# Scores of three attention units moved between the input products, and later row sums in a trunk kernel

## The chip, the cores and the metric

The kernel runs on one core of a Trainium2 chip. The metric is the device time of one execution in microseconds (us). The engines are named as in the profile: PE (TensorE), DVE (VectorE), ACT (ScalarE), POOL (GpSimd) and SP (SyncE, which here only issues transfers). Each works through its own queue in order; semaphores tie the queues together.

## The reference

Two layers of a trunk over 256 latent tokens x and 256 context tokens, width 1024. Each layer is a half-step SwiGLU, a token mixer and a second half-step SwiGLU; each sub-layer norms its input, shifts and scales it by values of a conditioning vector, norms its output and gates it.

```python
def _token_mixer(h, hc, ...):
    q, k, v, u, gb, gc, z = jnp.split(h @ w_in, SPLITS, axis=-1)
    ...                                              # kc, vc, uc: of the context tokens
    attn = _window_attention(q, k, v, kc, vc, sink)  # 8 heads, 2 of k and v, window 128, plus context
    ssm, ssm_c = _s5_mixer(u, uc, ...)               # diagonal scan, both directions, then a gated unit
    conv = gb * _short_conv(gc * z, conv_w)          # three taps
    y = jnp.concatenate([attn, ssm, conv], axis=-1) @ w_out
    if not ctx_out:                                  # the last layer
        return y, None
    ...                                              # the same for the context tokens
x = x + _gated_post(y, norm_post[l, 1], m[:, 5])
x = x + MACARON * _ffn_sublayer(x, m, 2, *f1)
```

All data and weights are float32.

## The kernel before

Values lie with the channels on partitions and the 512 tokens along the free axis: first the context (0 to 255), then x. Of each channel block there are 128 rows. A float32 product is made of three products in a reduced float32: each factor is split into a high part (`xh`, `wh`, a rounding copy on ACT) and a low part (`xl`, `wl`, a subtraction on DVE, or on POOL for the weights of w_out), and PE adds high by high, low by high and high by low (helper at L157, `mm3`). Weights come by transfers on SP into a ring of four buffers `wr` (`RAW`), and their two parts go into rings of six (`WB`). SP issues in order, so a transfer that waits for a free buffer holds all behind it.

The order of PE's instructions is the order of the program (a manual schedule for PE alone); on the other engines the framework's scheduler sets it. In the mixers the program's order is a table, `PROG`, of one string for each layer; the mixer function reads it step by step and calls a function for each. The letters are:

- `t10`, `t8`, `t9`, `t12`, `t11`, `t13`: half a product with w_in (for two blocks of output channels); each name stands twice, once for each half. ACT copies the result out (`wi`, L1247); t12 and t9, t11 and t13 give the convolution its parts (POOL L1275, L1277, L1283 and DVE L1279, L1281; result `cv`, then split).
- `u`, `U`: regroup the scan's input. `s0`, `s1`: the states of the scan's two halves (PE `pe` L1055, ACT copies `tx` L1059, POOL L1072 and L1084, DVE L1074 to L1091). `o0`, `o1`: read out the states (PE `py` L1110, with weights in buffers of the ring `wr`). `b0`, `b1`: back to channels, with a gelu. `g`: the gated unit of the scan (`pglu` L1147, weight `wglu` loaded by SP).
- `q`, `k`: split q or k in high and low part. `v`: transposes of v.
- `Sn`, `Tn`, `Vn`: attention of unit n. In the first mixer there are twelve units, three for each of four pairs of heads: two blocks of 128 x tokens and one for the context tokens (n = 2, 5, 8, 11). `S` is scores (PE L1170), the row maximum (`mx`, DVE L1181), its negative times the scale (`nm`), exponentials with sums (ACT L1194), the sink (`es`, ACT L1196), sums and reciprocal (DVE L1198, L1200) and the division (`P`, ACT L1202). `T` is the transposes of P (PE `pt` L1212) and two copies out of PSUM, the first on ACT, the second on DVE (`PT`, L1217 and L1215). `V` is the product with v (PE `O` L1228) and the split of its result.
- `wd`, `Wd`: load and split block d of w_out (the split on POOL). `edks`: the part of output block d from input block k, in token span s (context or x); the sum goes to PSUM `po`. `yd`: copy out and square. `x0`, `x1`: begin a norm and the residual. `z`: go one step further in the first span's chain (first a sum over the residual's squares by PE, `ss` L344, then its row factor `rb` L337 and the norm for the next SwiGLU).
- `r` (second mixer): one step of the row-wise part, among them transposes of x (`pxr` L439).

At the end of the first mixer the last two `z` are the sum over the squares of the residual x (`xacc` on DVE, `xsq` on ACT) and the row factor with the next SwiGLU's input. In the mixers P and most other values take a slot of a common pool of 39 (`SLOTS`).

Of the kernel before, what the change touches and what calls it, by code (L numbers as in the profile page):

```python
# [45 lines left out]
QSPLIT = (True, False)  # L46

PROG = (
# [13 lines left out]
)  # L62
QP = ()
LPF = 4
TORD = (ENG.Activation, ENG.DVE)
# [13 lines left out]
class Trunk:  # L79
# [1075 lines left out]
            cat[6 + half] = ch, cl  # L1155


    def attn_s(self, l, i, q, k, qt):
        nc = self.nc
        S = [self.ps("S") for _ in range(2)]  # L1160
        for part in ((qt,) if qt is not None else (0, 1)):
            for ab in range(2):
                pr = slice(64 * ab, 64 * ab + 64)
                if qt is not None:
                    o, qo = S[ab], CTX + qt * 128
                else:
                    o, qo = S[ab][:, part * 256:part * 256 + 256], part * 128
                xy = ((0, 0), (1, 0), (0, 1)) if len(q) > 1 else ((0, 0),)
                for n, (x, y) in enumerate(xy):
                    nc.tensor.matmul(o, q[x][pr, qo:qo + 128], k[y][pr, :o.shape[1]], start=n == 0,  # L1170
                                     stop=qt is None and n == len(xy) - 1, skip_group_check=True, tile_position=(64 * ab, 0))
        if qt is not None:
            c = 384 if qt == 0 else 256
            for ab in range(2):
                nc.tensor.matmul(S[ab][:, c:c + 128], self.identb, self.trib[:, qt], start=False, stop=True,
                                 skip_group_check=True)
        n = 1 if qt is not None else 2
        w = 512 // n
        mx = self.tiny("mx", 4)
        for ab in range(2):  # L1180
            nc.vector.tensor_reduce(mx[:, n * ab:n * ab + n], S[ab].rearrange("p (n k) -> p n k", n=n), axis=AX.X,  # L1181
                                    op=OP.max)

        sink = self.misc[:, l, 4 * i:4 * i + 2 * n] if n == 2 else self.misc[:, l, 4 * i:4 + 4 * i:2]
        cols = [slice(j, j + 1) for j in range(2 * n)]
        nm, es, sm = (self.tiny(t, 4) for t in ("nm", "es", "sm"))
        for c in cols:
            nc.vector.tensor_scalar(nm[:, c], mx[:, c], -SCALE, sink[:, c], op0=OP.mult, op1=OP.min)
        for c in cols:
            nc.vector.tensor_scalar(es[:, c], nm[:, c], sink[:, c], None, op0=OP.subtract)  # L1190
        Pm = [self.slot("P") for _ in range(2)]
        part = lambda j: Pm[j // n][:, j % n * w:j % n * w + w]
        for j in range(2 * n):
            nc.scalar.activation(part(j), S[j // n][:, j % n * w:j % n * w + w], AF.Exp, bias=nm[:, j:j + 1],  # L1194
                                 scale=SCALE, accum_out=sm[:, j:j + 1])
        nc.scalar.activation(es[:, :2 * n], es[:, :2 * n], AF.Exp)  # L1196
        for c in cols:
            nc.vector.tensor_scalar(sm[:, c], sm[:, c], es[:, c], None, op0=OP.add)  # L1198
        rd = self.tiny("rd", 4)[:, :2 * n]
        nc.vector.reciprocal(rd, sm[:, :2 * n])  # L1200
        for j in range(2 * n):
            nc.scalar.activation(part(j), part(j), AF.Copy, scale=rd[:, j:j + 1])  # L1202
        return Pm
# [33 lines left out]
    def mixer(self, l, H, pend, newH):  # L1237
        nc, a = self.nc, self.a
        last = l == NL - 1
        both = self.spans  # L1240
        lo = CTX if last else 0
        ev, cat = {}, {}
# [54 lines left out]
        u = [ev[0], ev[1]]  # L1297
        U, ut, vt = [], [], self.slot("vt")

        def vtok():  # L1300
            pv = self.pm("pvt")
            for tt in range(4):
                nc.tensor.transpose(pv[:, tt * 128:(tt + 1) * 128], ev[3][:, tt * 128:(tt + 1) * 128], self.ident)
            nc.scalar.activation(vt, pv, AF.Copy)
# [35 lines left out]
        qs, ks = {}, []  # L1340

        def qsplit(i):
            qs[i] = self.split(ev[4 + i], lo, T, pool=i in QP)

        def ksplit():
            ks.extend(self.split(ev[2], 0, T))

        wr, yr, us, q = {}, {}, [], []
# [25 lines left out]
        P, PT = {}, {}  # L1374

        def attn_s(n):
            i, qt = units[n]
            if not QSPLIT[last]:
                qs[i] = ev[4 + i],
            P[n] = self.attn_s(l, i, qs[i], ks if QSPLIT[last] else (ev[2],), qt)  # L1380

        def early_out(n):
            if last:
# [9 lines left out]
            v=lambda n: vtok(), k=lambda n: ksplit(), q=qsplit,  # L1393
            s=lambda n: S.append(self.ssm_states(l, n, U)), o=lambda n: yt.append(self.ssm_out(l, n, U, S[n], lo)),
            b=lambda n: G.append(self.ssm_back(yt[n], lo)), w=weight, r=lambda n: next(rows, None),
            g=lambda n: self.ssm_glu(l, G, cat, lo), e=early_out, x=tail if last else bound, S=attn_s,
            y=lambda n: oevac(n // 10, n % 10), z=lambda n: self.advance(out[0][1]), W=weight,
            T=lambda n: PT.update({n: self.attn_t(P.pop(n), units[n][1])}),
# [244 lines left out]
```

## Time and profile before

| | us |
|---|---|
| median of 3 runs | 1796.78 |
| lowest and highest run | 1795.67, 1804.11 |
| the profiled execution, its own time | 1789.94 |
| its span, first to last instruction | 1788.1 |

| engine | busy us | share of the span |
|---|---|---|
| PE | 1696.9 | 95% |
| DVE | 1111.6 | 62% |
| ACT | 687.6 | 38% |
| POOL | 728.3 | 41% |

The mean granted clock of PE is 0.982 of full speed (2.4 GHz). The share of busy time is a mean over all stages. The first mixer begins at 482.3 us of the span and ends at about 657.5, the second begins at about 1466; in between lie products of the SwiGLUs.

In a timeline a line has the start in us, the time in us, the engine, the line of the kernel, the operation, what it writes and reads, how many instructions are taken together, and in brackets how long the engine stood idle before it and what released it. A busy PE at half its clock counts as busy, so the granted clock stands in a view by stretch.

### The profile page before, as it was taken

The page shows a single profiled execution, that of the slowest core. Times are in us where ns is not written, and L with a number is a line of the kernel's source. Part 1 is how long each engine was busy: PE and PEld are TensorE (multiplying, and loading weights), DVE is VectorE, ACT ScalarE, POOL GpSimd, SP SyncE. Part 2 cuts the span into 40 slices and gives each one's busy share as a digit, 9 for nine tenths or more (in the row PEclk, how much of TensorE's full clock was granted, in tenths as well). Part 3 has the DMA queues.
Part 4 walks back from the last instruction along what each step waited for, and adds up shares of the span by engine and source line. Part 5 has one row for each costly group of instructions (what it writes and reads, how often), then busy time and mean ns, then how long its engine had stood idle before and what let it go on. Part 6 is the DMA issues. An engine that isn't in the chain of part 4 may idle for free.

```text
span 1788.1 us, 28686 instructions
## 1 busy us (share of the span) xinstructions
PE 1696.9 (95%) x11040; PEld 1449.6 (81%) x11040; DVE 1111.6 (62%) x2222; ACT 687.6 (38%) x1225; POOL 728.3 (41%) x651
## 2 busy tenths in 40 slices
PE   7999999999987989999999999999999989899998
PEld 5787777898975889787888989888888978579997
DVE  5798886827486466777774276765456476753223
ACT  4332322325337644323222244322222444655443
POOL 3100898955453143553438353000000563446552
PEclk9999999999998999999999999999999999999999
DMA  8676656644144032756664332646466443445662
GB/s 287 217 228 197 211 169 194 219 131 130 37 148 148 25 95 62 218 169 206 180 199 141 109 119 83 224 139 202 130 198 226 125 140 115 147 157 187 198 189 94
DMA packets 101688, 285.92 MB, mean 160 GB/s; under 512 B 19904, under 2 KB 27152, under 8 KB 101552
## 3 DMA queue, kind: packets, MB, share of 16 engines
q1 hardware_dynamic: 98960, 276.57, 49.1%
q0 software_dynamic: 2304, 7.46, 1.1%
q8 instruction: 86, 1.41, 0.3%
q14 instruction: 50, 0.41, 0.1%
q10 hardware_dynamic: 288, 0.07, 0.0%
HBM read 270.45 MB, written 15.70 MB: 160 GB/s over the span
## 4 chain that ended last, share of the span: by engine, by line
PE 79%; DVE 9%; issue 4%; DMA 4%; ACT 3%; POOL 1%; SPq 0%; DVEq 0%; ACTq 0%; POOLq 0%
PE pgu L157 39%; PE pd L157 18%; PE sk L157 8%; PE yr L497 4%; PE po L157 3%; DVE junk L252 2%; DVE wl L135 1%; DMA wr<-in_w_ada_dram 1%; PE pw L157 1%; PE ss L344 1%; DVE tn L370 1%; ACT wh L132 1%; POOL wl L135 1%; PE O L1228 1%; ACT hh L372 1%
## 5 line engine op out<-in xcount | busy, mean ns | idle before, releaser
L135 POOL TENSOR_TENSOR wl<-wr,wh 128x1024 fp32r<-128x1024 f32 (+1 forms) x140 | 327.8, 2359 | 674.9 <-ACT wh L132 324.6
L132 ACT ACTIVATE wh<-wr 128x1024 fp32r<-128x1024 f32 (+2 forms) x350 | 342.3, 983 | 594.5 <-PE pgu L157 166.4
L157 PE MATMUL pgu<-hh,wh 128*128 128x512 f32 (+1 forms) x1296 | 468.2, 361 | 0.0
L157 PE MATMUL pgu<-hl,wh 128*128 128x512 f32 (+1 forms) x1296 | 464.3, 358 | 0.0
L157 PE MATMUL pgu<-hh,wl 128*128 128x512 f32 (+1 forms) x1296 | 464.0, 358 | 0.0
L252 DVE SCALAR_TENSOR_TENSOR junk<-wr,sb 128x1024 bf16<-128x1024 f32 x224 | 314.4, 1404 | 161.3 <-DMA wr<-in_w_ada_dram 159.2
L135 DVE TENSOR_TENSOR wl<-wr,wh 128x1024 fp32r<-128x1024 f32 (+1 forms) x210 | 250.4, 1194 | 57.8 <-ACT wh L132 56.4
L157 PEld LDWEIGHTS pgu<-hh,wh 128*128 128x128 f32 x1296 | 244.3, 188 | 41.8 <-issue 1.7
L157 PEld LDWEIGHTS pgu<-hl,wh 128*128 128x128 f32 x1296 | 244.5, 189 | 40.4 <-issue 0.5
L157 PEld LDWEIGHTS pgu<-hh,wl 128*128 128x128 f32 x1296 | 244.2, 188 | 40.3
L157 PE MATMUL pd<-xh,wh 128*128 128x512 f32 (+1 forms) x696 | 241.8, 347 | 4.3 <-ACT xh L628 4.3
L157 PE MATMUL pd<-xl,wh 128*128 128x512 f32 (+1 forms) x696 | 237.4, 341 | 1.4 <-DVE xl L629 1.4
L157 PE MATMUL pd<-xh,wl 128*128 128x512 f32 (+1 forms) x696 | 237.2, 341 | 0.0
L157 PEld LDWEIGHTS pd<-xh,wh 128*128 128x128 f32 x696 | 131.6, 189 | 22.2 <-ACT xh L628 5.3
L157 PEld LDWEIGHTS pd<-xl,wh 128*128 128x128 f32 x696 | 132.0, 190 | 19.3 <-DVE xl L629 2.5
L157 PEld LDWEIGHTS pd<-xh,wl 128*128 128x128 f32 x696 | 131.6, 189 | 16.5
L157 PE MATMUL sk<-hl,wh 128*128 128x256 f32 x480 | 136.5, 284 | 6.8 <-DVE hl L375 6.8
L157 PE MATMUL sk<-hh,wh 128*128 128x256 f32 x480 | 137.5, 286 | 4.5 <-ACT hh L372 4.5
L157 PE MATMUL sk<-hh,wl 128*128 128x256 f32 x480 | 135.6, 283 | 0.0
L628 ACT ACTIVATE xh<-pgu 128x512 fp32r<-128x512 f32 (+1 forms) x61 | 35.1, 575 | 180.4 <-DVE pgu L627 180.3
L157 PEld LDWEIGHTS sk<-hl,wh 128*128 128x128 f32 x480 | 92.7, 193 | 8.4 <-DVE hl L375 8.3
L157 PEld LDWEIGHTS sk<-hh,wh 128*128 128x128 f32 x480 | 92.2, 192 | 6.2 <-ACT hh L372 6.1
(384 smaller groups left out, 2472.7 us busy)
## 6 DMA issues: line engine op xcount, KB each, us to landing
wr<-in_wgu_dram SPq DMA_DIRECT2D x170, 512.0 KB, 4.2
wr<-in_w_ada_dram SPq DMA_DIRECT2D x144, 512.0 KB, 4.3
wr<-in_wd_dram SPq DMA_DIRECT2D x72, 320.0 KB, 3.3
wr<-in_w_in_dram SPq DMA_DIRECT2D x32, 512.0 KB, 4.1
wr<-in_wd_dram SPq DMA_DIRECT2D x36, 448.0 KB, 3.9
wr<-in_wdr_dram SPq DMA_DIRECT2D x22, 512.0 KB, 3.7
wr<-in_w_out_dram SPq DMA_DIRECT2D x10, 512.0 KB, 4.2
V<-tvv POOLq DMA_DIRECT2D x16, 256.0 KB, 2.8
```

The source lines that it names most:

```text
L132: nc.scalar.activation(h[:, :cols], w[:, :cols], AF.Copy)
L135: eng.tensor_tensor(lo[:, :cols], w[:, :cols], h.bitcast(F32)[:, :cols], op=OP.subtract)
L157: mm = lambda a_, x_, st, sp: nc.tensor.matmul(po, a_[:, c], x_[:, lo:hi], start=st, stop=sp, skip_group_check=True)
L252: self.nc.vector.scalar_tensor_tensor(self.junk, w, 1.0, self.sb[:, s], op0=OP.mult, op1=OP.mult, accum_out=self.mod[l][:, m, b, s:s + 1])
L344: self.nc.tensor.matmul(p[:, b:b + 1], t[:, lo + b * 128:lo + (b + 1) * 128], self.rf[:, 0:1], start=first and b == 0, stop=last, skip_gro ...
L370: nc.vector.scalar_tensor_tensor(sc[d % 3], self.x[d][:, lo:hi], self.gs[l][s_][:, d, s:s + 1], rb[:, :hi - lo], op0=OP.mult, op1=OP.mult)
L372: nc.scalar.activation(H[d][0][:, lo:hi], sc[d % 3], AF.Identity, bias=bs[d])
L497: mm = lambda x_, a_, st, sp: self.nc.tensor.matmul(p, x_[:, c], a_[:, o:o + 512], start=st, stop=sp, skip_group_check=True)
L628: nc.scalar.activation(gh[:, lo:hi], pu, AF.Copy)
L1228: nc.tensor.matmul(O[pr, :w], vt[:, kt * 128 + 64 * ab:kt * 128 + 64 * ab + 64], PT[ab][:, kt * w:(kt + 1) * w], start=kt == 0, stop=kt == ...
```

## The change

The change edits the two strings, and gives three units of the first mixer tiles of their own for P.

```diff
 PROG = (
-    "q1 t10 u t10 U v t8 s0 t12 t8 t9 q0 q3 t11 k t12 s1 S2 w2 t9 t13 t11 t13 o0 S0 S5 T2 b0 q2 o1 V2 T5 w1 S1 b1 "
-    "T0 w0 V5 S8 V0 T1 S11 e000 e050 e040 S3 T8 e210 e250 e100 e150 e140 V1 e110 e010 V8 w3 g S4 T11 e220 e120 e260 "
+    "q0 t10 k u t10 U q1 S2 v t8 s0 t12 t8 S5 t9 T2 t12 q3 s1 V2 t9 w2 t11 t13 S0 t11 t13 T5 o0 V5 T0 b0 q2 S1 V0 "
+    "o1 w1 S8 b1 w0 T1 S11 e000 e050 e040 S3 T8 e210 e250 e100 e150 e140 V1 e110 e010 V8 w3 g S4 T11 e220 e120 e260 "
...
-    "e401 e451 e311 e471 e501 e331 z e131 e321 e121 e351 e251 e271 y71 e231 e261 e001 e211 y41 y51 z e161 e011 e151 "
-    "e101 y31 e171 y21 e111 e141 y11 e021 e051 e071 e031 e041 e061 y01 x1",
-    "t10 t8 S0 u t10 U S1 s0 r r t9 r r t8 r t12 v t12 t9 T0 S3 s1 S2 t11 T1 t11 V0 t13 t13 r r S4 r o0 S5 T2 S6 V1 "
+    "e401 e451 e311 e471 e501 e331 e131 e321 e121 e351 e251 e271 y71 e231 e261 e001 e211 y41 y51 z e161 e011 e151 "
+    "e101 y31 e171 y21 e111 e141 y11 e021 e051 z e071 e031 e041 e061 y01 x1",
+    "t10 t8 S0 u t10 U S1 s0 r r t9 t8 r r r t12 v t12 t9 T0 S3 s1 t11 T1 S2 t11 V0 t13 t13 r r S4 r o0 S5 T2 S6 V1 "
...
+EARLY = ({2: "bt", 5: "tws", 0: "bt"}, {})
...
-    def attn_s(self, l, i, q, k, qt):
+    def attn_s(self, l, i, q, k, qt, place=None):
...
-        Pm = [self.slot("P") for _ in range(2)]
+        Pm = [self.own(place, 2) if place else self.slot("P") for _ in range(2)]
...
-            P[n] = self.attn_s(l, i, qs[i], ks if QSPLIT[last] else (ev[2],), qt)
+            P[n] = self.attn_s(l, i, qs[i], ks if QSPLIT[last] else (ev[2],), qt,
+                               EARLY[last].get(n))
```

`self.own(place, 2)` gives a tile of the tag `place`, of which there are two buffers. Three parts can be told apart. (1) In the first mixer S2 stands behind U and q1, S5 and T2 among the products t9 and t12, V2 behind s1, S0 between t13 and t11, T5 ahead of o0, V5, T0 and V0 ahead of o1. (2) At the first mixer's end the third `z` stands ten part-steps later and the fourth nine, so that four are left behind it. (3) In the second mixer S2 stands behind the first t11 and T1, and two `r` stand behind the second t8. PE has 9144 instructions before and after.

Places where the order shows it. In the listings a row is the line, the operation, what it writes and reads (with buffer numbers), the shape and how many. Lines of the kernel after are 2 or 3 higher.

ACT in the first mixer, around the copies out of the products t11 and t13, the last of which is `wi_5303`; the rows with `P_5221` and `P_5222` are unit 2's exponentials and division, `yt_5323` is o0's. Before:

```order
L1194 ACTIVATE P_5221,sm_5212<-S_5193,nm_5210 128x256 x2
L1194 ACTIVATE P_5222,sm_5212<-S_5194,nm_5210 128x256 x2
L1247 ACTIVATE wi_5256<-pw_5035 128x512
L1247 ACTIVATE wi_5289<-pw_5062 128x512
L1247 ACTIVATE wi_5303<-pw_5258 128x512
L1202 ACTIVATE P_5221<-P_5221,rd_5232 128x256 x2
L1202 ACTIVATE P_5222<-P_5222,rd_5232 128x256 x2
L1115 ACTIVATE yt_5323<-py_5324 128x2x8x16
L142 ACTIVATE xh_5313<-cv_5306 128x512
```

After, where `wi_5400` is that last copy, `bt_5363` and `bt_5364` are unit 0's P, and `PT_5419` and `PT_5474` are ACT's copies of the transposes of units 5 and 0 (T5, T0):

```order
L1196 ACTIVATE bt_5363,sm_5358<-S_5343,nm_5356 128x512
L1196 ACTIVATE bt_5364,sm_5358<-S_5344,nm_5356 128x512
L1249 ACTIVATE wi_5386<-pw_5305 128x512
L1198 ACTIVATE es_5357<-es_5357 128x2
L1204 ACTIVATE bt_5363<-bt_5363,rd_5370 128x512
L1204 ACTIVATE bt_5364<-bt_5364,rd_5370 128x512
L1249 ACTIVATE wi_5400<-pw_5324 128x512
L1117 ACTIVATE yt_5434<-py_5435 128x2x8x16
L144 ACTIVATE xh_5410<-cv_5403 128x512
L1219 ACTIVATE PT_5419<-pt_5414 128x512
L1235 ACTIVATE ch_4788<-O_5462 128x256
L1219 ACTIVATE PT_5474<-pt_5469 128x512
```

The copy of t13 stood ahead of a division and now stands behind unit 0's exponentials and division; unit 5's copy stands behind the split `xh_5410` of the convolution made of it.

PE at the end of the first mixer, around the sum over the residual's squares (`ss`). Before:

```order
L157 MATMUL po_6377<-ch_4792,wh_5821 128x256
L157 MATMUL po_6377<-cl_4793,wh_5821 128x256
L157 MATMUL po_6377<-ch_4792,wl_5823 128x256
L344 MATMUL ss_6603<-rf,xacc_6483 128x1 x2
L344 MATMUL ss_6603<-rf,xsq_6484 128x1 x2
L157 MATMUL po_6629<-ch_4792,wh_6446 128x256
L157 MATMUL po_6629<-cl_4793,wh_6446 128x256
L157 MATMUL po_6629<-ch_4792,wl_6448 128x256
```

After, where `ss_6644` is that sum:

```order
L159 MATMUL po_6549<-ch_4788,wh_5301 128x256
L159 MATMUL po_6549<-cl_4789,wh_5301 128x256
L159 MATMUL po_6549<-ch_4788,wl_5303 128x256
L346 MATMUL ss_6644<-rf,xacc_6483 128x1 x2
L346 MATMUL ss_6644<-rf,xsq_6484 128x1 x2
L159 MATMUL po_6603<-xh_5832,wh_6446 128x256
L159 MATMUL po_6603<-xl_5833,wh_6446 128x256
L159 MATMUL po_6603<-xh_5832,wl_6448 128x256
```

The ten part-steps that stood behind the sum stand ahead of it, and e161, the first of the nine that stood behind the row factor, now follows it.

SP behind the last weights of the second mixer's output product (`in_w_outr`); `in_wgu` and `in_wdr` are weights of the SwiGLU that follows. Before:

```order
L125 DMA wr_15435<-in_w_outr_dram 128x1024
L125 DMA wr_15740<-in_wgu_dram 128x1024
L1143 DMA wglu_15375<-in_w_glu_dram 128x512
L125 DMA wr_15746<-in_wgu_dram 128x1024
L125 DMA wr_15812<-in_wdr_dram 128x1024
```

After:

```order
L127 DMA wr_15435<-in_w_outr_dram 128x1024
L127 DMA wr_15740<-in_wgu_dram 128x1024
L127 DMA wr_15746<-in_wgu_dram 128x1024
L1145 DMA wglu_15375<-in_w_glu_dram 128x512
L127 DMA wr_15812<-in_wdr_dram 128x1024
```

The load of `wglu` has moved behind the block `wr_15746` of the next SwiGLU's weights.

## Rows read from the trace of the kernel before

**Rows 1.** Timeline of PE in the first mixer; columns as told above.

```profile
520.83 0.58 PE L1170 MATMUL S<-xl,xh 64*128 64x256 f32 x1 [5.20 <-DVE xl L144]
...
534.80 0.44 PE L1110 MATMUL py<-wr,U 128*64 128x128 f32 x4
...
537.57 0.51 PE L1170 MATMUL S<-xh,xh 64*128 64x512 f32 x2
...
541.27 1.15 PE L1129 MATMUL pyt<-ident,yt 64*64 64x64 f32 x32 [0.29 <-DVE yt L1116]
...
549.86 1.97 PE L1228 MATMUL O<-PT,vt 128*64 128x256 f32 x8 [4.13 <-ACT PT L1217]
...
554.59 1.97 PE L1212 MATMUL pt<-ident,P 128*128 128x128 f32 x8 [2.75 <-ACT P L1202]
...
569.47 0.38 PE L157 MATMUL po<-ch,wh 128*128 128x256 f32 x1
...
575.60 0.37 PE L157 MATMUL po<-ch,wh 128*128 128x256 f32 x1
```

**Rows 2.** View by stretch: busy us of each engine, granted clock, DMA.

```profile
core 0: us, PE busy (x) PEld busy (x) DVE busy (x) ACT busy (x) POOL busy (x), PEclk, DMA share, GB/s
548.00:576.00 28.00, 18.75 (x148) 12.98 (x149) 16.82 (x64) 23.46 (x63) 11.76 (x5) 0.75 0.48 163
```

**Rows 3.** Timeline of DVE in the first mixer: states, splits, maximum.

```profile
500.57 1.29 DVE L1074 TENSOR_TENSOR pe<-pe,tvv 128x512 f32<-128x512 f32 x2
...
510.43 2.89 DVE L144 TENSOR_TENSOR xl<-wi,xh 128x512 fp32r<-128x512 f32 x1
...
520.09 0.68 DVE L144 TENSOR_TENSOR xl<-wi,xh 128x512 fp32r<-128x512 f32 x1
...
537.45 0.42 DVE L1091 TENSOR_TENSOR S<-tw,tz 64x256 f32<-64x256 f32 x1
...
541.92 1.28 DVE L1181 TENSOR_REDUCE mx<-S 128x1 f32<-128x512 f32 x2
```

**Rows 4.** Timeline of POOL there: a weight's low part, the convolution, w_out's weights.

```profile
509.92 2.85 POOL L135 TENSOR_TENSOR wl<-wr,wh 128x1024 fp32r<-128x1024 f32 x1
...
535.58 1.67 POOL L1275 TENSOR_TENSOR wi<-wi,wi 128x512 f32<-128x512 f32 x1 [1.93 <-ACT wi L1247]
...
537.35 1.88 POOL L1277 TENSOR_SCALAR cv<-wi,misc 128x512 f32<-128x512 f32 x1
...
544.14 1.27 POOL L1283 TENSOR_TENSOR cv<-cv,wi 128x512 f32<-128x512 f32 x1 [4.91 <-DVE nm L1188]
...
556.74 7.03 POOL L135 TENSOR_TENSOR wl<-wr,wh 128x1024 fp32r<-128x1024 f32 x3 [0.68 <-ACT wh L132]
```

**Rows 5.** Timeline of ACT there: states, copy of t13, division, a weight copy.

```profile
499.29 1.07 ACT L1059 ACTIVATE tx<-pe 128x512 f32<-128x512 f32 x2
...
534.91 0.60 ACT L1247 ACTIVATE wi<-pw 128x512 f32<-128x512 f32 x1 [0.68 <-PE pw L157]
...
550.76 1.36 ACT L1202 ACTIVATE P<-P,rd 128x512 f32<-128x512 f32 x2
...
559.84 1.06 ACT L132 ACTIVATE wh<-wr 128x1024 fp32r<-128x1024 f32 x1 [1.75 <-DMA wr<-in_w_out_dram]
```

**Rows 6.** Timeline of SP, and the page's DMA issues (us from issue to landing).

```profile
545.34 21.40 SPq L125 DMA_DIRECT2D wr<-in_w_out_dram  x9
...
wr<-in_w_out_dram SPq DMA_DIRECT2D x10, 512.0 KB, 4.2
```

**Rows 7.** Timeline of PE at the first mixer's end.

```profile
646.61 0.60 PE L344 MATMUL ss<-rf,xacc 128*128 128x1 f32 x4 [4.27 <-DVE xacc L357]
...
652.63 0.59 PE L337 MATMUL rb<-dg,rf 128*128 128x256 f32 x2
```

**Rows 8.** Timeline of PE in the second mixer.

```profile
1527.35 2.04 PE L1170 MATMUL S<-wi,wi 64*128 64x512 f32 x2 [5.10 <-DVE tpw L1075]
...
1531.92 1.03 PE L1212 MATMUL pt<-ident,P 128*128 128x128 f32 x8
...
1572.80 1.99 PE L1147 MATMUL pglu<-gelu,wglu 128*128 128x256 f32 x8 [0.31 <-DMA wglu<-in_w_glu_dram]
```

## The prediction

> **What bounds the kernel now.** I read the waits of TensorE first, then its timeline with the clock by stretch, and last the timelines of the engines that it waits for. Outside the mixers TensorE is fed almost without a gap, so only stretches in which it stands still can give time back. The first mixer has the largest one, from the scores of unit 2 to the dense stretch that begins with e210 at 575.60. In it TensorE waits 5.20 us inside unit 2's scores for VectorE's low part of k, 4.13 us at unit 2's product with V for a copy of its transposes, and 2.75 us at unit 5's transposes for its normalised P [rows 1]. Those waits also cost clock: from 548 to 576 us TensorE is busy for 18.75 of 28 us at a mean granted clock of 0.75 [rows 2]. At 2.4 GHz throughout that busy time would have been 18.75 x 0.75 = 14.1, so 4.7 us are due to the level of 1.2 GHz. Waits and clock of these rows come to 12.1 + 4.7, some 17 us: about what an order without these waits could win here. The work of TensorE is the same before and after, so it has nothing else to win.
>
> What feeds TensorE there is a chain on other engines. VectorE has hardly a gap from 500.57, where it takes up the first half of the states (s0), to 537.87, where the last of the states of s1 ends [rows 3]. Moving scores ahead on TensorE makes nothing of that work shorter; it changes what stands behind what.
>
> **Part 1, units 2, 5 and 0 between the products with w_in.** What it removes: the splits of k and q are wanted by a VectorE that was partly idle before 500 us, so unit 2's scores no longer meet the contended split (2.89 us beside a GpSimd subtraction, 0.68 alone [rows 3, 4]). I take off the whole 5.20 us and about 1 us of clock.
>
> What it adds, in the order of the path:
> (a) Unit 2's exponentials now stand ahead of the two copies tx of s0 on ScalarE, which began at 499.29 [rows 5]. The table load, four exponentials and a weight copy (1.06 us [rows 5]) ahead of them put tx, and so VectorE's start at 500.57, 3 to 4 us later. VectorE also gets unit 5's maximum inside this chain (1.28 us [rows 3]).
> (b) Unit 2's product V2 then stands right behind s1 on TensorE, while the VectorE copy that it needs stands behind s0's states. Before, VectorE did s0 and s1 with all that stood between in 37.3 us (500.57 to 537.87 [rows 3]), 18.6 each; since some splits now lie earlier I take 16 for s0 with unit 5's maximum. On from 504 the copy is there at 520. TensorE reaches V2 at about 515, where unit 2's scores stood still before (520.83 less 5.20 [rows 1]): it has one half product less ahead of it, and S2, S5 and T2 more, which cost about the same. It waits 5 us. That is the old 5.2 us in another place, with its clock.
> (c) The second half of the last product (t13) ended at 534.80 where the first read-out o0 begins. S0, S5 and T2, which took 3.4 us of TensorE behind o0 (537.57 to 541.27 less its 0.29 wait [rows 1]), now stand ahead of it, and V2 too with about 1 us at full clock (1.97 at half [rows 1]); unit 2's own scores cost what they did. The old wait is gone, the new one is as long, and the gain of clock takes some off: t13 ends at about 537.5, o0 with T5 at 541.
> (d) Now the step that decides. On ScalarE the copy of t13 out of PSUM (wi, 0.60 us at 534.91 [rows 5]) stands behind the exponentials and the normalisation of unit 0, as the order shows. Unit 0's maximum stands on VectorE behind s1's states, which end at 537.87 before [rows 3] and, with unit 5's 3 to 4 us added and the early splits taken off, at about 540 after. From there: maximum 1.28, small steps 0.6, two exponentials 1.3 and another copy 0.6, sums 0.5, normalisation 1.36, copy 0.6 [rows 3, 5]: it ends at about 546 instead of 535.5. Behind it stand the two GpSimd steps of the convolution (1.67 and 1.88), VectorE's part and the last GpSimd addition (1.27) [rows 4], the split of the result and only then unit 5's two copies. From the start of wi to the end of that addition it took 10.5 us before (534.91 to 545.41), of which GpSimd waited 4.91 for VectorE [rows 4, 5]; without that wait 5.6. Counted from the copy's start at 545.4 the addition ends at 551.0 to 555.9, nearer the lower end, since VectorE has little else by then; split and copies take 1.3. So V5 starts at 552 to 555 where TensorE is ready at 541: 11 to 14 us of wait, with the lower clock afterwards, in place of 4.13 + 2.75.
> (e) Then T0, b0, S1, V0 and o1 follow, some 9 us at a clock between the two levels, so o1 ends at 561 to 564. The weights of w_out wait for the buffers that o1 reads: SyncE put them out at 545.34 [rows 6], when o1 had ended. After, they go out at about 562, land 4.2 us later [rows 6], take a ScalarE copy of 1.06 each [rows 5], and two GpSimd subtractions of 7.03 / 3 = 2.34 us [rows 4]: e000 can start at 571 to 574, against 569.47 [rows 1]. T8 then finds its P ready, and e210 comes 4 us behind: 575 to 578, against 575.60 [rows 1]. **Sum of part 1: -0.6 to +2.4 by this working; I take +2**, nearer the upper end, since waits that I don't see can only add to such a queue. Bounds: -8 (rival 1) and +9.5 (rival 2).
>
> The tiles that EARLY gives to units 2, 5 and 0 I cost at nothing: T2, which frees the pair that unit 0 writes, stands well ahead of S0. If that cover went, the exponentials of S0 would wait for T2 and (d) would grow by as much.
>
> One more thing bears on (a) to (d). VectorE's split at 510.43 took 2.89 us, and it ended 0.55 us after GpSimd's subtraction had ended at 512.77; alone it takes 0.68 [rows 3, 4]. The Trainium skill, "SBUF — State Buffer", section "SBUF: two separate sides", says that VectorE with two inputs in SBUF and GpSimd hold their shared ports by turns for a whole instruction, and the other blocks. By that rule, the trace agrees at this place, and each further meeting would cost the sum up to 2.2 us, not a share of it.
>
> **Part 2, the sums and row steps at the end of the first mixer.** TensorE waits 4.27 us at the sum over xacc (646.61); ten part-steps lie between it and the row factor at 652.63, 6.0 us at partly the lower clock [rows 7]. After, the ten run ahead of the sum, in the old wait, and would cover it. But ScalarE's square xsq, on which the sum also rests, now stands behind two more weight copies of 1.06 us and two evacuations, so it comes some 3 us later. Nine other part-steps then lie between sum and row factor and cover VectorE's chain, which was as long as ten; only four are left ahead of the next products, which wait for the modulated x, as they did. Net: -0.5. Bounds: -3 (the wait goes and the second one doesn't grow) and +2.5 (xsq late and the last four steps don't cover).
>
> **Part 3, the second mixer.** The second half of unit S2's scores waits 5.10 us for a PSUM bank until 1527.35 [rows 8]. A half product (t11) and T1 are put ahead of it and lie in that wait. Before, they stood behind it, from 1529.39 to 1532.95, partly at the lower clock [rows 8]: up to -3.5. The row transposes that move behind the second half of t8 may leave a wait, too. What is late next: the weights behind o1, which the same VectorE chain holds, and w_glu, which on SyncE now stands behind one weight block that waits for GpSimd. TensorE waits 0.31 us for w_glu already [rows 8], so every us that its load goes out later is lost there. One GpSimd subtraction is 2.34 us [rows 4]. Net 0, bounds -3.5 and +2.5.
>
> **Sum.** +2 - 0.5 + 0 = +1.5 us. The profiled execution has 1789.94 us with a span of 1788.1; it is 6.8 us under the median of the runs shown, 1796.78, which I take for the measurement: 1798.3, so **1798 us**.
>
> **Rivals.**
> 1. *The waits go under cover* (faster). If VectorE reaches unit 0's maximum 5 us earlier than I count, or GpSimd and VectorE overlap the convolution fully, the ten us at V5 shrink to two, o1 ends at about 553 and the weights at 565: part 1 gives -8, with parts 2 and 3 at -0.5 and -2 some -10.5: 1786. For it speaks that VectorE had idle time before 500 us; against it that the copy of t13 stands in ScalarE's queue behind unit 0 whatever TensorE does.
> 2. *VectorE and GpSimd block each other more often* (slower). In the stretch from 500 to 538 one such meeting cost VectorE the 2.2 us above. With unit 5's softmax more on VectorE and the same GpSimd work in the stretch, two or three meetings more would bring unit 0's maximum 5 us later, V5 to 557 to 560, and TensorE's next 12 us of work at half clock cost up to 4 more: +2 + 5 + 2.5 = +9.5: 1806. It decides from about 4 us of added block. The Trainium skill's rule of the ports, on the same page, would give this time where GpSimd's steps of the stretch all meet VectorE's.
> 3. *The change does nothing here*: the weights of w_out are late by o1 alone, whatever stands ahead, and all waits shift by about a us: 1795 to 1797. It differs little from the forecast.
>
> **How the numbers follow.** My forecast and rival 3 together hold 0.72 (0.5 and 0.22), rival 1 holds 0.17, rival 2 holds 0.11. 0.5% is 9 us, about what a measurement of this kernel can tell from no change: faster means under 1787.8, slower over 1805.8. Rival 1's 1786 lies just beyond the one edge and rival 2's 1806 just beyond the other, so about 0.12 and 0.07 of them count there; 0.04 and 0.02 of my forecast do, by the bounds of parts 2 and 3. Faster 0.16, same 0.75, slower 0.09. The range takes in the times of both rivals, with 1 us more above for the bounds of the small parts: 1786 to 1807.
>
> **What would show it.** Right: no wait inside unit 2's scores; a wait of 4 to 6 us at V2 near 515 to 520; the copy of t13 near 545 and the longest wait, 9 us or more, at V5; the load of w_out's weights near 562; e000 between 570 and 575. The sum over xacc waits under 4 us. Wrong: if V5 waits less than 5 us, or e210 comes before 570, rival 1 holds; if VectorE's s1 ends after 545, rival 2. Part 3 is wrong if pglu waits over 3 us.

## The result, and the profile after

The changed kernel takes 1811.0 us (median of 9 runs, 1805.34 to 1812.66), the kernel before 1797.42 us beside it (9 runs, 1791.81 to 1804.11). The ratio is 1.0052, with an interval of 1.0034 to 1.0070: slower by 0.5%, or 9.4 us (6 to 13). The two medians lie further apart, 13.6 us; single runs of one kernel spread by up to 14 us, so I go by the ratio and its interval. I had forecast +1.5 us; the measured loss is that of rival 2 (+9.5), but, as the runs show, by another mechanism. On the 1796.78 us that the forecast started from, the ratio gives 1806.1: at the upper end of the range, and just over the 1805.8 from which I called it slower, with a chance of 0.09. The median itself lies beyond the 1807 of the range. By the profiles TensorE has 11040 MATMUL instructions before and after, so its work is the same.

The profiled execution of the kernel after has a span of 1807.4 us, 19.3 us more than the one of before. Not all of it is the change. I set landmarks on TensorE: the first mixer's first transposes (ut), e210, the row factor rb of the first span's first z step ("rb1"), the row factor of the second span ("rb2"), the second mixer's ut, the first ph of the part that follows, and the end.

| from, to | before | after | difference |
|---|---|---|---|
| start, first mixer's ut (not touched by the change) | 485.11 | 492.15 | +7.04 |
| ut, e210 | 90.49 | 97.06 | +6.57 |
| e210, rb1 | 56.89 | 59.94 | +3.05 |
| rb1, rb2 | 33.58 | 34.48 | +0.90 |
| rb2, second mixer's ut | 826.79 | 827.22 | +0.43 |
| that ut, first ph | 99.23 | 100.50 | +1.27 |
| first ph, end | 196.01 | 196.05 | +0.04 |

So 7 of 19.3 us come from before ut, where the change does nothing yet, and 9.6 from the first mixer's units. To compare a time of after with one of before in that mixer, take off 7.04.

The timeline of TensorE after, first mixer: V2, S0, T5, V5, b1, e000 (its first and its third product), e210, and pglu.

```profile
527.31 2.67 PE L1230 MATMUL O<-PT,vt 128*64 128x256 f32 x8 [5.17 <-ACT tws L1196]
...
539.51 0.51 PE L1172 MATMUL S<-xh,xh 64*128 64x512 f32 x2
...
546.20 1.03 PE L1214 MATMUL pt<-ident,tws 128*128 128x128 f32 x8
...
560.49 2.81 PE L1230 MATMUL O<-PT,vt 128*64 128x256 f32 x8 [10.48 <-ACT PT L1219]
...
575.34 1.15 PE L1131 MATMUL pyt<-ident,yt 64*64 64x64 f32 x32 [2.88 <-DVE yt L1118]
...
581.64 0.39 PE L159 MATMUL po<-ch,wh 128*128 128x256 f32 x1 [1.72 <-ACT wh L134]
...
584.07 0.58 PE L159 MATMUL po<-ch,wl 128*128 128x256 f32 x1 [1.93 <-POOL wl L137]
...
589.21 0.56 PE L159 MATMUL po<-ch,wh 128*128 128x256 f32 x1
...
597.17 5.28 PE L1149 MATMUL pglu<-gelu,wglu 128*128 128x512 f32 x8 [2.61 <-DMA wglu<-in_w_glu_dram]
```

Against [rows 1]: the 5.20 us inside unit 2's scores are gone, but V2 waits 5.17; the 4.13 and 2.75 us are gone, but V5 waits 10.48. The waits at b1, e000 and pglu are new.

How V5's wait comes about is read on ScalarE and GpSimd after. The ScalarE lines are the first of unit 0's two exponentials, its division (`bt<-bt,rd`), the copy of t13's second half (`wi`, at 552.59), the high part of the convolution (`xh`) and unit 5's copy `PT`; the GpSimd lines are the first and the last of its steps between that copy and `xh`:

```profile
548.66 0.69 ACT L1196 ACTIVATE bt<-S,nm 128x512 f32<-128x512 f32 x1 [7.76 <-DVE nm L1190]
...
551.35 1.33 ACT L1204 ACTIVATE bt<-bt,rd 128x512 f32<-128x512 f32 x2 [0.66 <-DVE rd L1202]
552.59 0.57 ACT L1249 ACTIVATE wi<-pw 128x512 f32<-128x512 f32 x1
...
559.32 0.63 ACT L144 ACTIVATE xh<-cv 128x512 fp32r<-128x512 f32 x1 [5.89 <-POOL cv L1285]
559.86 0.58 ACT L1219 ACTIVATE PT<-pt 128x512 f32<-128x512 f32 x1
```

```profile
553.24 1.27 POOL L1277 TENSOR_TENSOR wi<-wi,wi 128x512 f32<-128x512 f32 x1 [10.28 <-ACT wi L1249]
...
558.02 1.26 POOL L1285 TENSOR_TENSOR cv<-cv,wi 128x512 f32<-128x512 f32 x1 [1.85 <-DVE cv L1283]
```

TensorE had the last product of t13 done at 546.2, ScalarE was idle for 7.76 us while unit 0's maximum hung on VectorE, and the copy came 6.4 us late. VectorE after, the last step of s1's states and unit 0's maximum behind it:

```profile
546.37 0.42 DVE L1093 TENSOR_TENSOR S<-tc,tpw 64x256 f32<-64x256 f32 x1
...
547.16 1.28 DVE L1183 TENSOR_REDUCE mx<-S 128x1 f32<-128x512 f32 x2
```

What V5's wait hands on is read on SyncE after. The weights of w_out go out when o1 is done, at 571.15 - 7.04 = 564.1 against 545.34 in [rows 6]; w_glu stands behind all nine of them:

```profile
571.15 20.22 SPq L127 DMA_DIRECT2D wr<-in_w_out_dram  x9
591.42 0.43 SPq L1145 DMA_DIRECT2D wglu<-in_w_glu_dram  x1
```

And the cost of the clock, in the view by stretch, columns as in [rows 2]: the kernel before (first fence) and after (second). The first lines are 33 us that begin 22.9 us behind ut; the second are e000 to e210 and the third e210 to rb1, with the same work in both kernels.

```profile
508.00:541.00 33.00, 27.79 (x223) 21.97 (x221) 30.45 (x51) 11.93 (x26) 21.66 (x14) 0.90 0.32 103
569.47:575.60 6.13, 3.81 (x28) 2.51 (x26) 5.48 (x26) 5.62 (x22) 0.00 (x0) 1.00 0.15 57
575.60:632.50 56.90, 56.52 (x471) 47.97 (x469) 27.73 (x94) 34.69 (x85) 4.73 (x2) 0.97 0.07 20
```

```profile
515.00:548.00 33.00, 27.82 (x191) 21.24 (x191) 31.96 (x54) 9.83 (x24) 17.57 (x12) 0.90 0.26 88
581.64:589.21 7.57, 5.64 (x25) 4.46 (x26) 4.62 (x21) 7.57 (x20) 7.55 (x4) 0.61 0.70 196
589.21:649.15 59.94, 56.95 (x470) 47.47 (x469) 27.64 (x92) 34.00 (x84) 6.54 (x3) 0.96 0.14 42
```

From e000 to e210 TensorE is busy for 3.81 us at full clock before, and for 5.64 us at 0.61 after: 1.8 us are due to the clock. From e210 to rb1 it is busy for 56.52 and 56.95 us, at 0.97 and 0.96: there the loss of 3.05 us is the wait at pglu, not the clock. In the first 33 us the clock is 0.90 in both, and VectorE is busy for 30.45 us before and 31.96 after.

### The profile page after: what moved, and what is told of

It is laid out like the page before. It is cut to its first block, busy times and chain, and to the rows that moved or that the text cites. A ratio compares the mean times of both kernels' runs of the same rounds, so it can differ in the third digit from the quotient of the medians.

```text
span 1807.4 us, 28688 instructions
## 1 busy us (share of the span) xinstructions
PE 1701.5 (94%) x11040; PEld 1452.9 (80%) x11040; DVE 1114.7 (62%) x2222; ACT 688.1 (38%) x1225; POOL 726.9 (40%) x651
## 4 chain that ended last, share of the span: by engine, by line
PE 55%; DVE 5%; ACT 3%; issue 2%; DMA 1%; POOL 0%; DVEq 0%; ACTq 0%; SPq 0%
PE pgu L159 27%; PE pd L159 12%; PE sk L159 6%; PE yr L499 4%; PE po L159 2%; ACT wh L134 1%; DMA wr<-in_w_ada_dram 1%; DVE wl L137 1%; PE pt L1214 1%; PE O L1230 1%; PE S L1172 0%; PE ss L346 0%; PE pgu L552 0%; ACT hh L374 0%; DVE tn L372 0%
```

## The experiments

All landmarks are those of the table above, read from each run's own trace and counted from the first mixer's ut. "Front" is the first string up to S11. The front of before was run three times (before, e4, e11): e210 at 90.5, 89.6, 89.1 and rb1 at 147.4, 146.4, 144.4. That spread of 1.4 and 3.0 us is what a difference has to exceed. Each landmark comes from one execution; e5, e9 and e10 were run twelve times for their time, the others once.

**e1: part 1 alone.** The changed front and tiles; the other two edits undone.

```diff
-... e501 e331 e131 ... y41 y51 z e161 ... e021 e051 z e071 ...
+... e501 e331 z e131 ... y41 y51 z e161 ... e021 e051 e071 ...
-"t10 t8 S0 ... r r t9 t8 r r r t12 ... s1 t11 T1 S2 t11 ..."
+"t10 t8 S0 ... r r t9 r r t8 r t12 ... s1 S2 t11 T1 t11 ..."
```

> Part 1 alone; the ends of the first mixer and the second mixer as before. Distances on TensorE are from the first mixer's transposes ut. Theory (unit 0 in front of t13's copy, then o1, the weights and w_glu handed on): wait at V5 10 to 11 us, e210 97 us behind ut (before 90.5, after 97.1), the row factor of the first z-chain 157 (before 147.4, after 157.0). Rival (the stage also loses by the moved z or by the second mixer): under 95 and under 154.

Measured: V2 waits 5.3, V5 9.9, pglu 3.0 us; e210 at 95.8, rb1 at 154.1, between what the theory said (97 and 157) and the rival's marks (95 and 154). The kernel after, with the same front, has 97.1 and 157.0; the two differ by no more than the spread. The loss belongs to part 1: 154.1 against 144.4 to 147.4.

**e2: unit 0 behind t13's second half.**

```diff
-... w2 t11 t13 S0 t11 t13 T5 o0 V5 T0 ...
+... w2 t11 t13 t11 t13 S0 T5 o0 V5 T0 ...
```

> As e1, but unit 0's scores stand behind the second half of t13, so that ScalarE copies t13 out ahead of unit 0's exponentials. Theory: the wait at V5 falls from 10.5 to about 4.5 us (VectorE's states of s1 still hold the convolution), e210 stands 91 to 92 us behind ut. Rival (VectorE late by its own load, with or without that copy): V5 waits 9 us or more and e210 stays at 96 to 97.

Measured: V5's wait falls from 9.9 to 5.00, e210 comes at 90.1, rb1 at 148.3. ScalarE's timeline in e2 shows why: t13's copy is now ahead of the exponentials, right behind its product.

```profile
542.31 0.60 ACT L1249 ACTIVATE wi<-pw 128x512 f32<-128x512 f32 x1 [2.20 <-PE pw L159]
546.73 0.69 ACT L1196 ACTIVATE bt<-S,nm 128x512 f32<-128x512 f32 x1 [3.83 <-DVE nm L1190]
```

The theory holds and the rival falls: half of V5's wait was the place of one copy in ScalarE's queue. The rest is VectorE: in e2 its first step of the convolution begins at 546.93, behind the last of s1's states (until 544.87) and unit 0's maximum (545.24). pglu still waits 2.9 us in e2, and rb1 is no earlier than before.

**e3: o1 ahead of V5.**

```diff
-... T5 o0 V5 T0 b0 q2 S1 V0 o1 w1 S8 b1 w0 T1 S11
+... T5 o0 b0 q2 o1 w1 V5 T0 S1 V0 S8 b1 w0 T1 S11
```

> As e1, but o1 (with b0 and the loads of w1 and w0 around it) stands ahead of V5, so that the weights of w_out don't wait for V5. Theory: the wait at V5 stays (10 us less the 4 to 5 that o1 and b0 fill), but the weights go out some 13 us earlier, the waits at e000 and at w_glu go, e210 stands about 91 and the row factor about 148 behind ut. Rival (V5's wait costs by itself, the weights don't bind): e210 at 95 or more.

Measured: e210 at 86.9, rb1 at 143.5, no wait at e000 and none at pglu. SyncE in e3, where ut is at 486.98:

```profile
554.55 17.27 SPq L127 DMA_DIRECT2D wr<-in_w_out_dram  x9
571.86 0.42 SPq L1145 DMA_DIRECT2D wglu<-in_w_glu_dram  x1
```

The weights go out 67.6 us behind ut, in the changed kernel 79.0. The copy of t13 is as late as in e1 (60.6 us behind ut, there 60.2), and so is V5 (68.5 and 68.1), yet the whole loss is gone. V5's own wait is down to 0.53 us, since o1 and b0 (which waits 4.4 us) now lie ahead of it. So it isn't V5's lateness that costs, but that o1 stands behind it, and the weights behind o1. How much of the gain is the filled wait and how much the earlier weights, e3 alone doesn't separate.

**e4: part 2 alone** (the two `z` moved, all else as before).

```diff
-... e501 e331 z e131 ... y41 y51 z e161 ... e021 e051 e071 ...
+... e501 e331 e131 ... y41 y51 z e161 ... e021 e051 z e071 ...
```

> Part 2 alone (the two z later at the first mixer's end). Theory: the wait at the sum over xacc falls from 4.3 to about 2, another of about 2 at the next products' low part comes; from the first row factor of that end to that of the second span 33 to 34.5 us (before 33.6, after 34.5): no gain. Rival (the step alone gains, and was spoilt by part 1's clock): under 32.

Measured: the wait at the sum falls from 4.3 to 1.2 + 0.8 us, a new one of 2.1 comes at the next products' low part, and rb1 to rb2 takes 35.4 us. In e8, e12 and the changed kernel, which have this part too, it is 35.5, 35.0 and 34.5; in ten kernels without it 33.6 to 35.8. No gain. The changed kernel's own lines, to be held against [rows 7]:

```profile
663.72 0.60 PE L346 MATMUL ss<-rf,xacc 128*128 128x1 f32 x4 [1.18 <-DVE xacc L359]
665.10 0.89 PE L346 MATMUL ss<-rf,xsq 128*128 128x1 f32 x4 [0.77 <-ACT xsq L356]
...
674.55 0.39 PE L159 MATMUL sk<-hl,wh 128*128 128x256 f32 x1 [2.13 <-DVE hl L377]
```

The one run of e4 took 1811.1 us beside 1799.2 of before; its ut is at 497.78, 12.7 us later than in the profile of before, and from ut to the second ut it has 1011.1 us against 1007.8. Its time says little on part 2.

**e5: e2 and e3 together.**

```diff
-... w2 t11 t13 S0 t11 t13 T5 o0 V5 T0 b0 q2 S1 V0 o1 w1 S8 ...
+... w2 t11 t13 t11 t13 S0 T5 o0 b0 q2 o1 w1 V5 T0 S1 V0 S8 ...
```

> Part 1 with unit 0 behind t13's second half and o1 ahead of V5 together; the ends and the second mixer as before. Theory (two separate losses: the copy of t13 behind unit 0, and o1's late release of the weights): e210 84 to 87 us behind ut (o1 ahead alone 86.9, before 90.5 and 89.6), no wait for w_glu, and in time 0.1 to 0.4% faster than before. Rival (both moves cure the same loss, and the rest of part 1 loses elsewhere): e210 at 87 or more and no gain in time.

Measured: e210 at 88.3, rb1 at 144.4; in time 0.9982 of before (0.9963 to 1.0001). Against the forecast of e3's gain and more, the two moves don't add up: they cure the same loss, as the rival said. In its place T1 waits longer than in e3 (6.3 us against 4.8) and o1 waits for its own loads; V2's wait is as in e3. e5's waits of TensorE from 482 to 600 us (us in total, times, longest):

```profile
PE pt L1214 <- ACT P L1204: 6.3, 1, 6.3
PE O L1230 <- ACT tws L1196: 5.7, 1, 5.7
PE py L1112 <- DMA wr<-V: 2.1, 2, 1.4
```

**e6: e5 with V2 later.**

```diff
-... s1 V2 t9 w2 t11 t13 t11 ...
+... s1 t9 w2 t11 V2 t13 t11 ...
```

> As e5, with V2 two half products later, behind the first t11. Theory (VectorE's chain sets the pace): the wait of 5 to 6 us at V2 goes, TensorE is 5 us earlier at o0, but what follows waits that much longer: e210 within 1.5 us of e5. Rival (V2's wait is a loss by itself): e210 4 us or more earlier than e5.

Measured: V2 doesn't wait any more, and b0 waits 8.3 us in its place; the wait of 6 us at T1 stays. The product `pw` that now stands where V2 stood waits 2.1 us for unit 5's exponentials (`tws`). The same view of e6:

```profile
PE pyt L1131 <- DVE yt L1118: 8.3, 1, 8.3
PE pt L1214 <- ACT P L1204: 6.1, 1, 6.1
PE pw L159 <- ACT tws L1196: 2.1, 1, 2.1
```

e210 comes at 85.3, 3.0 us earlier than in e5 (I had allowed 1.5), but rb1 is the same, 144.5 and 144.4. The 3 us at e210 are lost again before rb1, where V1, for one, waits 2.2 us (0.8 in e5).

**e7: e5 with q2's and q3's low parts on GpSimd.**

```diff
-QP = ()
+QP = (3, 2)
```

> As e5, with the low parts of q2 and q3 made by GpSimd in place of VectorE, two subtractions of 0.68 us less on VectorE. Theory (VectorE's chain sets the pace, and GpSimd blocks it when they meet): e210 0 to 1.4 us earlier, less where GpSimd's subtraction meets VectorE. Rival (VectorE isn't the bound): no change, or later by GpSimd's longer subtraction.

Measured: e210 at 88.9, rb1 at 144.7: no change, as the rival said, though the theory's 0 to 1.4 us is no more than the spread. Two subtractions less on VectorE buy nothing that can be seen; which of its other steps would, these runs don't tell.

**e8: the changed kernel with P in the common pool.**

```diff
-EARLY = ({2: "bt", 5: "tws", 0: "bt"}, {})
+EARLY = ({}, {})
```

> The changed kernel with P of units 2, 5 and 0 in the common pool of slots, as before. Theory: the tiles of their own cost and give nothing: the waits at V2 and V5 stay at 5 and 10 us, e210 96 to 97 and the first row factor 154 to 157 behind ut. Rival (the second pair's wait for T2 or the pool's slots matter): e210 off by 2 us or more.

Measured: V5 waits 7.8 in place of 10.5, b1 0.8 in place of 2.9, e210 comes at 93.2, rb1 at 151.8 (with the tiles 97.1 and 95.8, 157.0 and 154.1). The program's order is the same; what differs is the scheduler's order on ScalarE, as its timeline in e8 shows: the copy of t13 is ahead of unit 0's division.

```profile
551.17 0.60 ACT L1249 ACTIVATE wi<-pw 128x512 f32<-128x512 f32 x1
551.94 1.33 ACT L1204 ACTIVATE P<-P,rd 128x512 f32<-128x512 f32 x2 [0.17 <-DVE rd L1202]
```

In the kernel after the copy follows the division. I had costed the tiles at nothing; here they stand for 2.5 to 4 us at e210, on one run of e8 against the two with the tiles: the rival's "2 us or more".

**e9: e3 with the common pool.**

```diff
-EARLY = ({2: "bt", 5: "tws", 0: "bt"}, {})
+EARLY = ({}, {})
```

> As e3 (o1 ahead of V5, ends and second mixer as before), with P of all units in the common pool. Theory (the tiles of their own cost through the order that they give ScalarE; o1's place is the rest of the loss): e210 83 to 87 us behind ut, the first row factor 141 to 144 (before 147.4 and 146.4), in time 0.1 to 0.4% faster than before. Rival (e8's gain of some 3 us was the spread between executions): same as e3, 86.9 and 143.5, and in time within 0.2%.

Measured: e210 at 89.7, rb1 at 146.1, in time 0.9997 of before (0.9982 to 1.0011). Not better than e3 (86.9, 143.5), and at e210 not the same either: 2.8 us later, against e8's 2.5 to 4 us earlier. In time the rival holds. Once o1 is ahead, the common pool wins nothing; what the tiles cost depends on what stands around them, and one run of each kind doesn't settle its size.

**e10: e9 with T1 behind e040.**

```diff
-... b1 w0 T1 S11 e000 e050 e040 S3 T8 ...
+... b1 w0 S11 e000 e050 e040 T1 S3 T8 ...
```

> As e9, with T1 behind the first three part-steps (e000 to e040), since unit 1's P came late in e3 and e5 (waits of 4.8 and 6.3 us at T1). Theory (the next bound is the order of ScalarE and VectorE behind the weights): the wait at T1 falls under 2 us, the first row factor is 1 to 3 us earlier than in e9. Rival (it is the pace of VectorE and ScalarE as a whole): the wait moves to the next transposes and the row factor stays within 1 us of e9.

Measured: the wait of 6.1 us at T1 shrinks to 2.0, e000 comes 8 us earlier, and rb1 at 145.8 against 146.1; in time 1.0001 of before (0.9985 to 1.0016). The rival again: the wait taken from one place isn't a gain at the end of the stage.

**e11: part 3 alone** (the changed second string, all else as before).

```diff
-"t10 t8 S0 ... r r t9 r r t8 r t12 ... s1 S2 t11 T1 t11 ..."
+"t10 t8 S0 ... r r t9 t8 r r r t12 ... s1 t11 T1 S2 t11 ..."
```

> Part 3 alone. Theory (VectorE's chain sets the pace there too): the wait of 5.1 us in S2's scores turns into one of 5.2 us at T1, and from the second mixer's ut to the first ph it takes 99 to 100.5 us (before 99.2; kernels with the second mixer as before 99.0 to 100.3): no change. Rival (part 3 saves 3 us alone): 97 or less.

Measured: 99.8 us from ut to ph (in the ten kernels with the old second mixer 99.0 to 100.3). The three that have the other parts too (after, e8, e12) take 100.5, 100.8 and 100.5, just above that range; e11 alone doesn't show this loss. The wait of 5.1 in S2's scores [rows 8] is gone, and one of 5.2 stands at T1, in e11 as in the kernel after. After, on TensorE and on ScalarE:

```profile
1545.21 2.21 PE L1214 MATMUL pt<-ident,P 128*128 128x128 f32 x8 [5.22 <-ACT PT L1219]
```

```profile
1543.89 0.20 ACT L1198 ACTIVATE es<-es 128x2 f32<-128x2 f32 x1 [4.77 <-DVE es L1192]
...
1544.57 0.59 ACT L1219 ACTIVATE PT<-pt 128x512 f32<-128x512 f32 x1
```

T1 waits for a buffer that ScalarE's copy of T0's transposes frees; that copy stands behind an exponential that waits 4.77 us for VectorE. S2's scores hung on VectorE, too (`tpw` in [rows 8]).

**e12: the changed kernel with w_glu's load put out early**, at b0, ahead of w_out's nine, in both mixers.

```diff
+        def glu_load():
+            self.wg = self.slot("wglu")
+            nc.sync.dma_start(self.wg, a["w_glu"][l])
...
-            b=lambda n: G.append(self.ssm_back(yt[n], lo)), w=weight,
+            b=lambda n: (G.append(self.ssm_back(yt[n], lo)), n or glu_load()), w=weight,
...
-        wg = self.slot("wglu")
-        nc.sync.dma_start(wg, self.a["w_glu"][l])
+        wg = self.wg
```

> The changed kernel with the first and the second mixer's load of w_glu put out at b0, ahead of the weights of w_out in SyncE's order. Theory (the last 3 us of the loss ahead of the first row factor are w_glu's load, held behind the nine loads of w_out, and the clock behind that wait): the wait at pglu (2.6 us in the changed kernel) goes, e210 stays at 96 to 97 us behind ut, and the first row factor comes at 153 to 155 in place of 157.0. Rival (what precedes pglu is bound elsewhere, another wait takes its place): the row factor stays within 1 us of 157.

Measured: no wait at pglu, e210 at 96.3, rb1 at 151.8, against 157.0 (after) and 154.1 (e1). The gain is 2.3 to 5.2 us, all of it behind e210. From e210 to rb1 the four kernels in which pglu waits (after, e1, e2, e8) take 58.3 to 59.9 us; e12 takes 55.5, and all others but e6 (59.2, with V1's wait) 55.3 to 56.9. So the second term of the loss is w_glu's load, held by SyncE's order: 2.8 to 4.4 us, e12 against e1 and after.

## Why the prediction was right and wrong

**Right, with its sizes: the places of the waits.** Off 7.04 us, the kernel after has:

| step | forecast | measured |
|---|---|---|
| wait inside unit 2's scores | none | none |
| (a) GpSimd's first work on tx, later by | 3 to 4 | 2.65 (509.64 less 7.04 against 499.95) |
| (b) V2: begins, waits | 520, 5 | 520.3, 5.17 |
| (c) t13 ends, TensorE ready for V5 | 537.5, 541 | 539.2, 543 |
| (d) s1's states end | 540 | 539.8 |
| (d) copy of t13 begins | 545.4 | 545.6 |
| (d) convolution's last addition ends | 551.0 to 555.9 | 552.2 |
| (d) V5: begins, waits | 552 to 555, 11 to 14 | 553.4, 10.48 |
| (e) w_out's weights go out | 562 | 564.1 |
| (e) e000 | 571 to 574 | 574.6, its low part 577.0 |
| (e) e210 | 575 to 578 | 582.2 |

Following each queue by hand, with durations from the trace, gave the times of four engines up to e000, over 70 us, to within about 2 us. Two steps hid a wrong reason. In (b) I had V2 wait for VectorE's copy of unit 2's transposes. That copy ended 0.6 us after V2 began; the wait ended with unit 5's exponentials on ScalarE, which read a bank of the PSUM pool that V2's `O` comes from. Both hang on VectorE's work for s0, so the number came out right:

```profile
526.71 0.46 ACT L1196 ACTIVATE tws<-S,nm 128x256 f32<-128x256 f32 x1
```

```profile
527.26 0.69 DVE L1217 COPY PT<-pt 128x512 f32<-128x512 f32 x1
```

And in (c) I took 1.7 us off t13's end for a gain of clock, which didn't come (0.90 in both, see the view by stretch); without it the terms give the measured 539.2.

**Wrong: step (e), the tail of part 1.** I let e210 come 4 us behind e000; it took 7.6. The weight's copy on ScalarE stood behind unit 8's exponentials, its low part came 1.93 us after TensorE wanted it, and the stretch ran at a granted clock of 0.61, behind waits of 10.48, 2.88 and 1.72 us (its products with w_out last 0.41 to 0.58 us each from 584 to 589, against 0.28 at full clock). I had counted the four us from a stretch of before with a wait of 2.3 us in it, and took that wait off without putting on the new wait (1.93 us) and the clock (1.8 us): term (e) was too small by about 4 us.

**Wrong: a queue that I didn't follow to its end.** The sum stopped at e210. But w_glu stands behind the nine weights of w_out on SyncE, as it did before; when those went out 18.8 us later, so did it, and pglu waited 2.61 us. I named w_glu as the next late thing, but in the second mixer, where pglu doesn't wait in the kernel after. e12 shows the price in the first: 2.8 to 4.4 us. Together the two missed terms, about 4 us and about 3, make up most of the difference between my +2 for part 1 and the measured +9.6 (against the three fronts of before: after +9.6 to +12.7, e1 +6.7 to +9.7).

**Wrong: the tiles of EARLY at nothing.** The cover that I named (T2 ahead of S0) held. But the tiles changed the order on ScalarE (e8), which I had seen as a fact of the order and not as an effect of that edit. What this costs stays open: 2.5 to 4 us in e8, the other way round in e9.

**Rivals.** Rival 2's time came true, its mechanism not: its mark was s1's states ending after 545, and they ended at 539.8. That VectorE and GpSimd blocked each other more often is not what the loss was: from the first step of s0's states to the last of s1's VectorE took 36.5 us, against 37.3 before. That the loss came out at rival 2's +9.5 is luck. (The meeting of 2.2 us that I priced there is the largest of several: in the kernel before a step at 513.92 takes 1.53 us beside GpSimd's at 513.90, where one of the same shape at 516.49 takes 0.41.) Rival 1 wanted V5's wait under 5 us; e2 and e3 show what it would have taken, and that it ends level with before, not 10 us ahead. Rival 3 was nearest in spirit: w_out's weights did hang on o1 alone. It missed that o1 would now stand behind V5.

**Part 2** was right in its mechanism (xsq behind two more weight copies, 2.0 us later behind rb1 where I had said 3; four part-steps too few): forecast -0.5, measured +0.9, within the spread. **Part 3**: forecast 0, measured +1.3 in the kernel after, 0.2 us beyond the range of the kernels without it, and in e11 +0.1 against their mean; its new wait was at T1, not at w_glu, and I had not followed T0's copy on ScalarE.

**What stays open.** In e3, e5 to e7, e9 and e10 the waits are in different places, yet rb1 comes at 143.5 to 146.1 in all, and with before's front at 144.4 to 147.4. That VectorE and ScalarE together set that pace fits e6 and e10, and VectorE's 31.96 of 33 us; that e7 gained nothing speaks, if anything, against VectorE alone. It isn't shown: no run made either engine's work in this stretch much less. No version beats the kernel before by more than the measurement tells; e5, at 0.9982 (0.9963 to 1.0001), comes nearest.

## What to carry to other kernels

Work that is moved ahead on the engine with the most to do moves ahead on the queues of the others, too, and pushes something back there: look for what now stands behind it, above all a short copy that a long chain hangs on. Follow the lateness to the last queue that it reaches, the transfers behind the transfers included; the sum ends where no queue is late any more, not where the moved work ends. When TensorE is on time only if another engine is, taking a wait from one place puts it at the next (V2, b0, T1 here), so ask for each wait what the releaser would do next before you count it as gain.

## What the runs showed of the hardware

The stretch ahead of the first mixer, which no kernel changes, took 485.1 to 497.8 us in the 14 profiled executions. In the longest, e4, the view by stretch shows TensorE with a granted clock of 0.66 and 13.31 of 20 us busy between 280 and 300 us, where the kernel before has 0.94 and 20.00 (e12, with 497.3 us the next longest, has 0.66 and 13.36):

```profile
280.00:300.00 20.00, 13.31 (x102) 10.04 (x103) 8.80 (x13) 5.19 (x11) 12.82 (x12) 0.66 0.56 148
```

The last stretch, from the first ph to the end, took either 196.0 to 196.3 us (six executions) or 200.2 (eight), and nothing in between, whatever the kernel. TensorE's waits in it come to 0.8 to 1.0 us in all of them, and the granted clock is 1.00 in both kinds; TensorE is busy for 187.1 us in the kernel after and for 191.4 in e10, with as many products, so its products themselves take longer. Why isn't known. Both together would be enough to set single runs of one kernel up to 14 us apart, though those runs have no trace that shows it; distances between landmarks leave both out.
